# A macaron encoder layer on one core: the moved sums and split remainders of both FFNs, and half of three quarters of a modulation product

## The chip, the cores and the metric

The kernel runs on one core of a Trainium2 chip. The metric is the device time of one execution in microseconds (us); lower is better. Five engines work side by side, each through its own list of instructions in order: PE (TensorE, matrix products), DVE (VectorE), ACT (ScalarE), POOL (GpSimd) and SP (SyncE, which issues most transfers). An engine that waits for something holds up all that stands behind in its own list.

## The reference

One encoder layer over 1024 tokens of width 1024, all in float32:

```python
c_act = silu(c)
mod = c_act @ w_ada + b_ada                 # nine vectors of 1024: shift, scale, gate for three blocks
h = modulate(rms_norm(x, g_ffn1), sh_f1, sc_f1)
x = x + 0.5 * gt_f1 * swiglu(h, w1_gu, w1_down)     # FFN 1, width 2816
h = modulate(rms_norm(x, g_mix), sh_m, sc_m)
...                                          # two attentions with 8 heads each
x = x + gt_m * (o @ w_out)
h = modulate(rms_norm(x, g_ffn2), sh_f2, sc_f2)
x = x + 0.5 * gt_f2 * swiglu(h, w2_gu, w2_down)     # FFN 2
return rms_norm(x, g_final)
```

where `swiglu(h) = (silu(a) * b) @ w_down` with `a, b` the halves of `h @ w_gu`.

## The kernel before

**Precision.** A float32 product is made of three faster ones: each operand is split in a high part (ACT casts it, `Stream.split` L105 or `split_b` L461) and the remainder (a subtraction, L106 or L462), and PE multiplies high by high, high by low and low by high (L485 to L487 in the gate and up products, L741 to L743 in the down products). So every 128x512 block that PE uses first passes ACT once and DVE or POOL once.

**FFN.** The gate and up products run unit by unit (22 units of 128 columns, `GateUp`), each as a two by two block product with seven block products in place of eight. On the weight side that takes the sums S1 to S4 (`unit_specs`, L426; S1 and S3 on POOL, S2 and S4 on DVE), on the side of the activations the sums T1 to T4 (`build`, L468, L470, L473, L476; the first of each part, L468 and L473, on POOL) and remainders (L462; those of B22 and T4 on POOL). For the down product, the gated results of a pair of units are written to DRAM blocks `g_d` by `g_out`, among them three or four sums on POOL (L521); the ones named A... are stored through SP and the ones named S... through POOL's own transfer queue (L517). Of the 22 units, 8 are early: two of their products (A11 with B11, A12 with B21, 24 matrix instructions a unit) are made ahead, while the activations are still being built (`early`, `early2`, `early_rest`); the other five follow in `run`.

**Order of the work.** `Stream` holds a list of weight loads with the steps on them (sums and splits); `pump(n)` takes the next n steps, with 9 split pairs and 2 raw buffers of 1 MB at a time. `Background` steps generators. The order in which the source issues work is not the order on the engines: a scheduler places each instruction in its engine's list.

**First modulation.** Before FFN 1 can start, its shift and scale are needed: `w_ada01` comes in four quarters q of 2 MB, in two loads each (`raw01`, four buffers). `use01` (L795) multiplies each of eight slices with its value of `cact` and adds it into `acc01[q]` on DVE; `prepare1` (L922) then sums over the partitions with four matrix products against a column of ones into `modp`, from which DVE makes `modB` and `modA` (L926, L927), ACT modulates (L911) and splits, and PE can go on with that quarter. `acc_new` (L894, L895) clears the next accumulator on POOL, once PE has read the buffer's last content, and fetches a row of biases through ACT's queue.

**From gate and up to down.** When `run` ends, the buffers of `gu_pools` are given up and the down product's tiles take their place: the gate row (L397) and x (L990 in FFN 1, L1610 in FFN 2) can be loaded only when the last stores from the old buffers are through. The down product's first operand, A12, is read back from `g_d` in three chunks (L95, `raw<-g_A`), through the same SP list.

Of the kernel before, what the change touches and what calls it, by code (L numbers as in the profile page):

```python
# [19 lines left out]
ALU = mybir.AluOpType  # L20
# [4 lines left out]
P = 128  # L25
D = 1024
S = 1024
KT = D // P
# [155 lines left out]
def encoder_layer(ctx: ExitStack, tc: tile.TileContext, a: dict, out: bass.AP):  # L184
    nc = tc.nc
# [10 lines left out]
    st = Stream(nc, rawp, ring)  # L196
# [42 lines left out]
    ones = const.tile([P, P], F32, name="ones")  # L239
# [5 lines left out]
    cact = const.tile([P, KT], F32, name="cact")  # L245
# [170 lines left out]
    def unit_specs(i, u, early):  # L416

        src = a[f"w{i}_gu"][u // 2, u % 2]
        A = [slice(j * 512, (j + 1) * 512) for j in range(4)]
        tmps = {}  # L420

        def comb(nm, eng, x, y, op):
            def f(raw):
                tmps[nm] = sp.tile([P, 512], F32, tag="S", name="S")
                get = lambda v: tmps[v] if isinstance(v, str) else raw[:, A[v]]
                eng.tensor_tensor(tmps[nm], get(x), get(y), op=op)  # L426
            return f

        def blk(nm, v):
            if isinstance(v, str):  # L430
                return ((i, u, nm), None, lambda raw: tmps[v])
            return ((i, u, nm), A[v], None)

        direct = not early
        steps = [comb("S1", nc.gpsimd, 2, 3, ALU.add), comb("S3", nc.gpsimd, 0, 2, ALU.subtract)]
        if direct:
            steps.append(blk("A11", 0))
        steps += [comb("S2", nc.vector, "S1", 0, ALU.subtract), blk("S2", "S2"), blk("S1", "S1"), blk("S3", "S3")]
        if direct:
            steps.append(blk("A12", 1))  # L440
        steps += [comb("S4", nc.vector, 1, "S2", ALU.subtract), blk("S4", "S4"), blk("A22", 3)]
        return [(src, steps)]
# [3 lines left out]
    class GateUp:  # L446
# [17 lines left out]
        def build(self, hf, kk, part):  # L464

            b11, b21, b12, b22 = hf[0][:, kk, :], hf[0][:, kk + 4, :], hf[1][:, kk, :], hf[1][:, kk + 4, :]
            if part == 0:
                nc.gpsimd.tensor_tensor(b11, b12, b11, op=ALU.subtract)  # L468
                self.split_b("T1", kk, b11, nc.vector)
                nc.vector.tensor_tensor(b11, b22, b11, op=ALU.subtract)  # L470
                self.split_b("T2", kk, b11, nc.vector)
            else:
                nc.gpsimd.tensor_tensor(b12, b22, b12, op=ALU.subtract)  # L473
                self.split_b("T3", kk, b12, nc.vector)
                self.split_b("B22", kk, b22, nc.gpsimd)
                nc.vector.tensor_tensor(b21, b21, b11, op=ALU.subtract)  # L476
                self.split_b("T4", kk, b21, nc.gpsimd)

        def prod(self, p, u, wn, bn, kks, start, stop):
            wh, wl = st.get((self.i, u, wn))  # L480
# [31 lines left out]
        def g_out(self, fp, nm):  # L512

            g = self.g

            def put(nm):
                (nc.sync if nm[0] == "A" else nc.gpsimd).dma_start(g_d[nm][:, fp, :], g[nm])  # L517

            def comb(nm, x, y, op, into=None):
                g[nm] = gtp["g"]() if into is None else g[into]  # L520
                nc.gpsimd.tensor_tensor(g[nm], g[x], g[y], op=op)  # L521
                put(nm)

            if nm != "A21":
                put(nm)
            if nm == "A11":
                comb("S3", "A11", "A21", ALU.subtract)
            if nm == "A22":
                comb("S1", "A21", "A22", ALU.add, "A21")
                comb("S2", "S1", "A11", ALU.subtract, "A11")  # L530
                comb("S4", "A12", "S2", ALU.subtract, "A12")
# [18 lines left out]
        def early_rest(self, builds):  # L550

            K4 = (0, 1, 2, 3)
            for u0 in range(NQ0, NE, 4):
                us = range(u0, u0 + 4)
                for u in us:
                    self.bank[u] = ps1()
                    self.prod(self.bank[u], u, "A11", "B11", K4, True, True)
                    self.store_p1(u)
                    next(builds, None)
                    st.pump(2)  # L560
                    bg.step()
                for u in us:
                    self.prod(self.bank[u], u, "A12", "B21", K4, False, True)
                    self.early_out(u)
                    next(builds, None)
                    st.pump(2)
                    bg.step()
            for _ in builds:
                pass
# [219 lines left out]

    acc01 = {}  # L790

    def use01(q, kt):
        def use(raw):
            ac = acc01[q]
            nc.vector.scalar_tensor_tensor(out=ac, in0=raw[:, kt % 4 * 512:(kt % 4 + 1) * 512], scalar=cact[:, kt:kt + 1],  # L795
                                           in1=ac, op0=ALU.mult, op1=ALU.add)
        return use
# [63 lines left out]
    x = [xs.tile([P, D], F32, name=f"x{t}") for t in range(NT)]  # L861
# [37 lines left out]
    modp = p1p.tile([P, 512], F32, tag="ps1", name="modp")  # L899
# [14 lines left out]
    def prepare1(q):  # L914
        if q == 1:
            for t in range(4, 8):
                bg.spawn(start_gen(t))
                bg.step()
        st.upto(ends01[q] + (1 if q < 2 else 0))
        p = modp[:, 4 * q:4 * q + 4]  # L920
        for m in range(4):
            nc.tensor.matmul(p[:, m:m + 1], acc01[q][:, m * P:(m + 1) * P], ones[:, 0:1], start=True, stop=True)  # L922
        if q < 2:
            acc_new(q + 2)
        ks = slice(2 * q, 2 * q + 2)
        nc.vector.tensor_copy(modB[0][:, ks], p[:, 0:2])  # L926
        nc.vector.scalar_tensor_tensor(out=modA[0][:, ks], in0=p[:, 2:4], scalar=1.0,  # L927
                                       in1=cols[:, C_GF1 + 2 * q:C_GF1 + 2 * q + 2], op0=ALU.add, op1=ALU.mult)
        for k in (2 * q, 2 * q + 1):
            modulate(0, k)  # L930
            ffn.split_b("B11" if k < 4 else "B21", k % 4, hf[0][:, k, :], nc.vector)
        if q == 3:
            bg.finish()
            ss_.close()
            R2.append(rs.enter_context(tc.tile_pool(name="R2", bufs=1, side="right")))
            ffn.alloc(R2[0], T_NAMES)
            st.hold, st.hold_step = hold_u0 + 1, hold_u0


            def builds():  # L940
                for part in range(2):
                    for kk in range(4):
                        if part == 0:
                            modulate(1, kk)
                            modulate(1, kk + 4)
                        ffn.build(hf, kk, part)
                        yield

            return builds()
# [33 lines left out]
    x = [dp.tile([P, D], F32, name=f"x{t}") for t in range(NT)]  # L983
# [45 lines left out]
    for t in range(NT):  # L1029
        bg.finish(norms[t])  # L1030
        p = in_proj(t, "b", 256)
# [391 lines left out]
    for s in range(NQ + LAG + 3):  # L1423
        if s < NQ:
            i, t = divmod(s, NT)
            p = scores(i, t)
# [304 lines left out]
```

## Time and profile before

| | |
|---|---|
| median of 3 runs | 2048.51 us (2046.16 to 2048.94) |
| profiled execution, its own time | 2049.28 us |
| its span | 2047.5 us |
| mean granted clock of TensorE | 0.988 of full speed |
| PE busy | 1971.7 us (96%) |
| DVE busy | 1540.1 us (75%) |
| ACT busy | 973.4 us (48%) |
| POOL busy | 483.7 us (24%) |

The shares are averages over stages of different kinds: FFN 1 until about 700 us, the projections and attentions until about 1380, FFN 2 to the end. What a change is worth in one of them is read from that stage: where PE has no gap, work on another engine is hidden, and where PE waits, the last wait counts. [...]

### The profile page before, as it was taken

The numbers are of one execution on the slowest core, as the hardware profiler recorded it, in microseconds if no ns is written. First come the engines' busy times: TensorE is split into PE (matmuls) and PEld (weight loads), VectorE is DVE, ScalarE is ACT, GpSimd is POOL, SyncE is SP. The second block draws the span as 40 slices with busy tenths as digits, with TensorE's granted clock in tenths as the row PEclk, the third lists the DMA queues.
The fourth block names the chain that finished last, engine by engine and source line by source line (L and its number), as shares of the span: only waits on it lengthen the run. The fifth ranks groups of instructions, "written<-read, shape, count | busy, mean of one in ns | idle before, by whom it ended". The sixth has DMA issues, their size and how long they took to land. (4 is left out here: it accounts for less than half of the span.)

```text
span 2047.5 us, 28023 instructions
## 1 busy us (share of the span) xinstructions
PE 1971.7 (96%) x10301; PEld 1678.1 (82%) x10301; DVE 1540.1 (75%) x2381; ACT 973.4 (48%) x1865; POOL 483.7 (24%) x428
## 2 busy tenths in 40 slices
PE   6889999999999999999999999998999999999998
PEld 5678888887788888798989998996788888877886
DVE  7898689886697776788888778667776555547976
ACT  6522322322344653677787777467323333324444
POOL 1544344433000032212200000005343332320011
PEclk9999999999999999999999999998999999999999
DMA  8275366565832334523253330433442332358223
GB/s 344 88 246 186 106 202 216 197 223 187 334 116 93 147 123 143 156 63 118 89 165 83 83 75 30 164 127 126 165 163 100 113 118 83 113 207 322 98 93 118
DMA packets 90550, 303.30 MB, mean 148 GB/s; under 512 B 9848, under 2 KB 22427, under 8 KB 76588
## 3 DMA queue, kind: packets, MB, share of 16 engines
q1 hardware_dynamic: 81018, 274.21, 39.8%
q0 software_dynamic: 7040, 23.07, 2.9%
q10 hardware_dynamic: 2354, 4.22, 0.5%
q8 instruction: 81, 1.33, 0.3%
q14 instruction: 57, 0.47, 0.1%
HBM read 220.98 MB, written 80.49 MB: 147 GB/s over the span
## 5 line engine op out<-in xcount | busy, mean ns | idle before, releaser
L105 ACT CAST uh<-raw 128x512 fp32r<-128x512 f32 (+1 forms) x343 | 210.4, 622 | 228.8 <-PE ps L486 148.1
L106 DVE TENSOR_TENSOR ul<-raw,uh 128x512 fp32r<-128x512 f32 (+1 forms) x343 | 250.3, 735 | 41.1 <-ACT uh L105 40.7
L105 ACT CAST uh<-S 128x512 fp32r<-128x512 f32 x198 | 121.6, 621 | 302.3 <-PE ps L486 234.7
L741 PE MATMUL ps<-uh 128*128 128x512 f32 x616 | 240.8, 393 | 7.3 <-ACT uh L105 7.3
L742 PE MATMUL ps<-ul,uh 128*128 128x512 f32 x616 | 241.5, 392 | 1.7 <-DVE ul L106 1.7
L743 PE MATMUL ps<-uh,ul 128*128 128x512 f32 x616 | 240.9, 391 | 0.0
L1428 DVE TENSOR_REDUCE nm<-ps 128x1 f32<-128x1024 f32 x128 | 155.7, 1216 | 70.6 <-PE ps L223 40.9
L106 DVE TENSOR_TENSOR ul<-S,uh 128x512 fp32r<-128x512 f32 x198 | 168.8, 858 | 41.8 <-ACT uh L105 41.6
L521 POOL TENSOR_TENSOR g<-g 128x512 f32<-128x512 f32 x88 | 135.1, 1535 | 244.3 <-DVE g L508 243.3
L1446 ACT CAST ph<-ps 128x512 fp32r<-128x512 f32 x256 | 138.0, 590 | 79.6 <-PE ps L1445 79.4
L426 POOL TENSOR_TENSOR S<-raw 128x512 f32<-128x512 f32 x88 | 123.4, 1414 | 200.3 <-DMA raw<-in_w_gu_dram 122.5
L1456 DVE TENSOR_TENSOR pl<-ps,ph 128x512 fp32r<-128x512 f32 x256 | 163.9, 683 | 0.0
L1451 ACT ACTIVATE pe<-ps,nm 128x1024 f32<-128x1024 f32 x128 | 143.6, 1122 | 17.2 <-DVE nm L1428 17.1
L741 PEld LDWEIGHTS ps<-uh 128*128 128x128 f32 x616 | 116.1, 189 | 33.2 <-ACT uh L105 9.0
L742 PEld LDWEIGHTS ps<-ul,uh 128*128 128x128 f32 x616 | 116.4, 189 | 27.7 <-DVE ul L106 3.8
L743 PEld LDWEIGHTS ps<-uh,ul 128*128 128x128 f32 x616 | 116.3, 189 | 24.2
L1445 PE MATMUL ps<-ident,pe 128*128 128x128 f32 x1024 | 134.9, 273 | 0.8 <-DVE pl L1456 0.4
L1445 PEld LDWEIGHTS ps<-ident,pe 128*128 128x128 f32 x1024 | 119.7, 141 | 19.0 <-DVE pl L1456 0.6
L105 ACT CAST uh<-hT 128x512 fp32r<-128x512 f32 x96 | 59.7, 622 | 150.4 <-PE ps L742 113.5
L1394 PE MATMUL po<-ph,V 128*128 128x256 f32 x512 | 129.7, 291 | 0.0
L1395 PE MATMUL po<-pl,V 128*128 128x256 f32 x512 | 125.9, 283 | 0.0
L233 POOL TENSOR_TENSOR r<-v,neghalf 128x1 f32<-128x1 f32 x32 | 26.0, 813 | 363.8 <-DVE v L229 363.8
(280 smaller groups left out, 5178.0 us busy)
## 6 DMA issues: line engine op xcount, KB each, us to landing
raw<-in_w_gu_dram SPq DMA_DIRECT2D x52, 1024.0 KB
ada<-in_w_ada_dram SPq DMA_DIRECT2D x56, 512.0 KB
g_S<-g POOLq DMA_DIRECT2D x88, 256.0 KB, 2.6
g_A<-g SPq DMA_DIRECT2D x66, 256.0 KB
hT<-in_w_down_dram SPq DMA_DIRECT2D x16, 1024.0 KB
raw<-g_S SPq DMA_DIRECT2D x16, 1024.0 KB
raw<-g_A SPq DMA_DIRECT2D x12, 1024.0 KB
x<-in_x_dram SPq DMA_DIRECT2D x16, 512.0 KB
```

The costliest lines, as they stand in the source:

```text
L105: nc.scalar.copy(hi[:, 0:n], ap)
L106: nc.vector.tensor_tensor(lo[:, 0:n], ap, f32(hi[:, 0:n]), op=ALU.subtract)
L521: nc.gpsimd.tensor_tensor(g[nm], g[x], g[y], op=op)
L741: nc.tensor.matmul(p, gh[:, tsl], wh, start=start, stop=False, skip_group_check=True)
L742: nc.tensor.matmul(p, gh[:, tsl], wl, start=False, stop=False, skip_group_check=True)
L743: nc.tensor.matmul(p, gl[:, tsl], wh, start=False, stop=stop, skip_group_check=True)
L1394: nc.tensor.matmul(po[:, 0:256], V, gr.ph[:, k, :], start=(k == 0), stop=False)
L1428: nc.vector.tensor_reduce(nm, p, axis=AX.X, op=ALU.max, negate=True)
L1445: nc.tensor.transpose(out=pt[:, k, :], in_=pe[:, (4 * n + k) * P:(4 * n + k + 1) * P], identity=ident)
L1446: nc.scalar.copy(gr.ph[:, 4 * n:4 * n + 4, es], pt)
L1451: nc.scalar.activation(pe, p, AF.Exp, bias=nm, accum_out=ls[:, s % 2:s % 2 + 1])
L1456: nc.vector.tensor_tensor(gr.pl[:, nsl, es], pts[n], f32(gr.ph[:, nsl, es]), op=ALU.subtract)
```

## The change

1. The sums S1 and S3 (L426), the sums of `g_out` (L521), the first sums of `build` (L468, L473) and the remainders of B22 and T4 (L462) move from POOL to DVE. POOL keeps clearing tiles, the powers of `inv_rms`, its stores and what it does in the attentions.
2. In `early_rest`, the step on the weights (`st.pump(2)`) comes ahead of the step on the activations (`next(builds, None)`).
3. Of quarters 1 to 3 of the first modulation, DVE adds up the first four slices only. For the last four a new function `mod_matmuls` multiplies the raw block by four columns of `cact` on PE (16 products of 128x128 by one column), with the four products against ones in between. The buffers `raw01` are given back by PE there, not by DVE.

```diff
-        steps = [comb("S1", nc.gpsimd, 2, 3, ALU.add), comb("S3", nc.gpsimd, 0, 2, ALU.subtract)]
+        steps = [comb("S1", nc.vector, 2, 3, ALU.add), comb("S3", nc.vector, 0, 2, ALU.subtract)]
...
             if part == 0:
-                nc.gpsimd.tensor_tensor(b11, b12, b11, op=ALU.subtract)
+                nc.vector.tensor_tensor(b11, b12, b11, op=ALU.subtract)
...
             else:
-                nc.gpsimd.tensor_tensor(b12, b22, b12, op=ALU.subtract)
+                nc.vector.tensor_tensor(b12, b22, b12, op=ALU.subtract)
                 self.split_b("T3", kk, b12, nc.vector)
-                self.split_b("B22", kk, b22, nc.gpsimd)
+                self.split_b("B22", kk, b22, nc.vector)
                 nc.vector.tensor_tensor(b21, b21, b11, op=ALU.subtract)
-                self.split_b("T4", kk, b21, nc.gpsimd)
+                self.split_b("T4", kk, b21, nc.vector)
...
                 g[nm] = gtp["g"]() if into is None else g[into]
-                nc.gpsimd.tensor_tensor(g[nm], g[x], g[y], op=op)
+                nc.vector.tensor_tensor(g[nm], g[x], g[y], op=op)
...
                     self.store_p1(u)
+                    st.pump(2)
                     next(builds, None)
-                    st.pump(2)
...
                     self.early_out(u)
+                    st.pump(2)
                     next(builds, None)
-                    st.pump(2)
...
+    def mod_matmuls(q, raw=None):
+
+        for m in range(4):
+            ms = slice(m * P, (m + 1) * P)
+            o = modp[:, 4 * q + m:4 * q + m + 1]
+            if raw is not None:
+                for j in range(4):
+                    nc.tensor.matmul(o, raw[:, j * 512:(j + 1) * 512][:, ms], cact[:, 4 + j:5 + j], start=j == 0, stop=False)
+            nc.tensor.matmul(o, acc01[q][:, ms], ones[:, 0:1], start=raw is None, stop=True)
+
     def use01(q, kt):
         def use(raw):
+            if q and kt >= 4:
+                if kt == KT - 1:
+                    mod_matmuls(q, raw)
+                return
...
-        for m in range(4):
-            nc.tensor.matmul(p[:, m:m + 1], acc01[q][:, m * P:(m + 1) * P], ones[:, 0:1], start=True, stop=True)
+        if q == 0:
+            mod_matmuls(0)
```

The scheduler places other instructions anew as well. Three places show it. First, PE's list behind the first twelve products of FFN 1 (`ps_268` is the second unit's bank, `modp` the modulation's, `ps_345` takes transposed x). Before:

```order
L487 MATMUL ps_268<-B11h_128,ul 128x512
L922 MATMUL modp<-ones,acc 128x1 x4
L882 MATMUL ps_345<-ident,xn 128x128 x4
L485 MATMUL ps_269<-B11h_128,uh 128x512
```

With the change:

```order
L487 MATMUL ps_268<-B11h_128,ul 128x512
L799 MATMUL modp<-cact,raw_177 128x1 x4
L800 MATMUL modp<-ones,acc 128x1
L799 MATMUL modp<-cact,raw_177 128x1 x4
L800 MATMUL modp<-ones,acc 128x1
L799 MATMUL modp<-cact,raw_177 128x1 x4
L800 MATMUL modp<-ones,acc 128x1
L799 MATMUL modp<-cact,raw_177 128x1 x4
L800 MATMUL modp<-ones,acc 128x1
L896 MATMUL ps_345<-ident,xn 128x128 x4
```

Twenty products stand where four stood. They stand again in front of the quarters 2 and 3; in quarter 2 the last six products of the unit before and four groups of transposes moved behind them.

Second, DVE's list while FFN 2's activations are built (T1l to T4l and B22l are remainders, `hT` the sums, `eg` an early unit's result, which frees a bank for PE). Before, between the second and the third `eg`:

```order
L508 TENSOR_TENSOR eg<-ps_14637,es 128x512
L462 TENSOR_TENSOR T2l_14598<-hT,T2h_14597 128x512
L106 TENSOR_TENSOR ul<-raw,uh 128x512
L462 TENSOR_TENSOR T3l_14600<-hT,T3h_14599 128x512
L462 TENSOR_TENSOR T3l_14602<-hT,T3h_14601 128x512
L476 TENSOR_TENSOR hT<-hT 128x512 x2
L426 TENSOR_TENSOR S<-S,raw 128x512
L426 TENSOR_TENSOR S<-raw,S 128x512
L462 TENSOR_TENSOR T3l_14602<-hT,T3h_14601 128x512
L106 TENSOR_TENSOR ul<-S,uh 128x512 x4
L106 TENSOR_TENSOR ul<-raw,uh 128x512
```

With the change, the end of that stretch:

```order
L462 TENSOR_TENSOR T3l_14638<-hT,T3h_14637 128x512
L462 TENSOR_TENSOR B22l_14626<-hT,B22h_14625 128x512
L462 TENSOR_TENSOR T4l_14642<-hT,T4h_14641 128x512
L476 TENSOR_TENSOR hT<-hT 128x512
L426 TENSOR_TENSOR S<-raw 128x512 x2
L462 TENSOR_TENSOR T4l_14642<-hT,T4h_14641 128x512
L426 TENSOR_TENSOR S<-S,raw 128x512
L508 TENSOR_TENSOR eg<-ps_14827,es 128x512
L426 TENSOR_TENSOR S<-raw,S 128x512
L106 TENSOR_TENSOR ul<-S,uh 128x512 x4
L106 TENSOR_TENSOR ul<-raw,uh 128x512
```

The remainders and sums from POOL stand between the others, and the third `eg` now stands ahead of the five splits that it stood behind.

Third, SP's list where FFN 2 goes from the gate and up products to the down product (`g_A_93` is A12, `g_A_92` A11). Before:

```order
L86 DMA hT<-in_w_down_dram 128x2048
L397 DMA gate<-gd 128x1024
L1610 DMA z_17968<-xd_91 128x1024
L1610 DMA z_17969<-xd_91 128x1024
L1610 DMA z_17970<-xd_91 128x1024
L1610 DMA z_17971<-xd_91 128x1024
L95 DMA raw<-g_A_93 128x1536
L95 DMA raw<-g_A_92 128x2048
```

With the change:

```order
L86 DMA hT<-in_w_down_dram 128x2048
L95 DMA raw<-g_A_93 128x1536
L397 DMA gate<-gd 128x1024
L1624 DMA z_18004<-xd_91 128x1024
L1624 DMA z_18005<-xd_91 128x1024
L1624 DMA z_18006<-xd_91 128x1024
L1624 DMA z_18007<-xd_91 128x1024
L95 DMA raw<-g_A_92 128x2048 x2
```

The third chunk of A12 moved from behind the gate row and four rows of x to ahead of them; in FFN 1 it moved in the same way.

## Rows read from the trace of the kernel before

**Rows 1.** Windows: us, then each engine's busy time (instructions), PEclk, DMA share, GB/s.

```profile
50.00:100.00 50.00, 40.20 (x155) 30.00 (x156) 44.69 (x47) 31.55 (x56) 27.48 (x18) 0.90 0.21 75
100.00:150.00 50.00, 43.60 (x184) 35.10 (x184) 45.30 (x54) 12.38 (x22) 20.71 (x18) 0.96 0.71 243
150.00:480.00 330.00, 330.00 (x1471) 271.57 (x1470) 270.74 (x328) 101.08 (x171) 137.65 (x112) 1.00 0.57 190
...
496.00:530.00 34.00, 29.69 (x121) 22.94 (x120) 19.96 (x28) 14.04 (x26) 7.83 (x8) 0.95 0.84 316
...
1396.00:1450.00 54.00, 43.66 (x169) 34.30 (x168) 48.48 (x47) 27.62 (x52) 33.82 (x22) 0.87 0.34 118
...
1450.00:1820.00 370.00, 370.00 (x1634) 306.35 (x1634) 223.25 (x316) 111.58 (x183) 127.82 (x119) 1.00 0.35 121
...
1820.00:1852.00 32.00, 27.32 (x110) 21.15 (x109) 18.60 (x26) 13.00 (x24) 7.51 (x8) 0.95 0.82 312
```

**Rows 2.** Shorter windows in the first modulation and FFN 2's building stage, same columns.

```profile
51.00:57.00 6.00, 5.12 (x11) 3.23 (x12) 5.89 (x7) 3.94 (x7) 3.76 (x3) 0.51 0.11 44
...
1423.00:1428.00 5.00, 5.00 (x12) 3.94 (x13) 5.00 (x4) 1.45 (x3) 4.06 (x3) 0.50 0.77 254
1431.00:1436.00 5.00, 5.00 (x22) 4.17 (x23) 5.00 (x5) 3.60 (x7) 4.37 (x3) 1.00 0.33 99
1442.00:1446.40 4.40, 4.40 (x12) 3.46 (x13) 1.30 (x3) 0.03 (x1) 1.88 (x2) 0.61 0.65 251
```

**Rows 3.** Timeline, PE: start, duration, instruction, in brackets idle time before.

```profile
51.84 1.65 PE L485 MATMUL ps<-B21h,uh 128*128 128x512 f32 x3 [2.82 <-ACT B21h L461]
...
84.58 0.79 PE L487 MATMUL ps<-B21h,ul 128*128 128x512 f32 x1 [3.91 <-DVE ul L106]
...
1422.98 0.79 PE L485 MATMUL ps<-B21h,uh 128*128 128x512 f32 x1 [6.21 <-ACT c L493]
...
1847.62 0.50 PE L741 MATMUL ps<-uh 128*128 128x512 f32 x1 [3.32 <-ACT uh L105]
```

**Rows 4.** Timeline, DVE in FFN 2's building stage.

```profile
1398.25 2.65 DVE L106 TENSOR_TENSOR ul<-raw,uh 128x512 fp32r<-128x512 f32 x2 [9.02 <-ACT uh L105]
...
1408.23 0.68 DVE L462 TENSOR_TENSOR T1l<-hT,T1h 128x512 fp32r<-128x512 f32 x1
...
1413.19 1.78 DVE L462 TENSOR_TENSOR T1l<-hT,T1h 128x512 fp32r<-128x512 f32 x1
...
1432.74 5.78 DVE L106 TENSOR_TENSOR ul<-S,uh 128x512 fp32r<-128x512 f32 x4
...
1439.64 0.68 DVE L508 TENSOR_TENSOR eg<-ps,es 128x512 f32<-128x512 f32 x1
```

**Rows 5.** Costliest groups: line, instruction, count | busy us, mean ns | idle before.

```profile
L106 DVE TENSOR_TENSOR ul<-S,uh 128x512 fp32r<-128x512 f32 x198 | 168.8, 858 | 41.8 <-ACT uh L105 41.6
L521 POOL TENSOR_TENSOR g<-g 128x512 f32<-128x512 f32 x88 | 135.1, 1535 | 244.3 <-DVE g L508 243.3
...
L426 POOL TENSOR_TENSOR S<-raw 128x512 f32<-128x512 f32 x88 | 123.4, 1414 | 200.3 <-DMA raw<-in_w_gu_dram 122.5
```

**Rows 6.** Timelines of DVE, PE and POOL in the first modulation.

```profile
18.77 2.49 DVE L106 TENSOR_TENSOR ul<-raw,uh 128x512 fp32r<-128x512 f32 x4
...
29.39 1.03 PE L922 MATMUL modp<-ones,acc 128*128 128x1 f32 x8
...
30.48 0.52 POOL L894 MEMSET acc<- 128x512 f32 x1 [9.12 <-PE modp L922]
```

**Rows 7.** Timeline, SP (issue times), and the transfers of 1826 to 1850.

```profile
1835.84 1.11 SPq L95 DMA_DIRECT2D raw<-g_A  x2
...
DMA packets 1612, 7.46 MB, mean 311 GB/s; under 512 B 208, under 2 KB 208, under 8 KB 1232
```

**Rows 8.** Waits of POOL and DVE: us in total, times, longest.

```profile
POOL S L426 <- DMA raw<-in_w_gu_dram: 122.5, 18, 11.7
...
DVE acc L313 <- DMA ada<-in_w_ada_dram: 11.1, 6, 4.3
```

## Prediction

> **What bounds the kernel now.** I read the windows first, because a share over the whole execution mixes stages. In the steady part of both FFNs PE works without a gap: 330.00 of 330 us from 150 to 480 and 370.00 of 370 us from 1450 to 1820, at clock 1.00, while DVE and POOL both have idle time [rows 1]. Whatever another engine does there is hidden. PE loses time only at the edges of these runs. From 50 to 150 it is idle 9.80 + 6.40 = 16.20 us, from 1396 to 1450 it is idle 10.34 us, and at the two passages from gate and up to down (496 to 530, 1820 to 1852) 4.31 and 4.68 us. In these windows DVE is busy for 44.69 of 50, 45.30 of 50 and 48.48 of 54 us [rows 1], so there it is nearly a bound itself.
>
> A gap costs more than its length. [...] I count the missing clock of a window as lost time too: 5.00 x 0.50 = 2.5 us there, 4.40 x 0.39 = 1.7 us from 1442, 6.00 x 0.49 = 2.9 us from 51 to 57 [rows 2].
>
> Next, why DVE is slow there. The timeline shows the same remainder (T1l) with 0.68 us at 1408.23 and 1.78 us at 1413.19, and four splits of S in 5.78 us at 1432.74 [rows 4], where four splits early in the program take 2.49 us [rows 6], 0.62 each. POOL's sums take 1414 and 1535 ns each over the whole execution, and the splits of S 858 ns on average [rows 5]. So both engines read as slower while both work. One sum moved to DVE takes some 1.4 us from POOL, adds 0.62 us to DVE, and takes away a neighbour that makes DVE's own work nearly three times as long.
>
> **The change part by part.** The sum is made against the profiled execution's 2049.28 us, which is 0.77 above the median.
>
> *Steady runs: 0.* With everything on DVE, 328 + 112 instructions x 0.62 = 273 of 330 us and 316 + 119 x 0.62 = 270 of 370 us [rows 1, 6] (an upper estimate, as some of POOL's instructions stay). DVE stays under 85%, and what hides its work is PE's full list. If DVE were held up there by over 15% of the stage, PE would run dry; that is rival D.
>
> *FFN 2's building stage (1396 to 1450): -12.* PE can gain 10.34 us of idle time and 2.5 + 1.7 of clock, 14.5 in all. DVE's list up to the third `eg` has 40 instructions in the new order; at 0.62 that is 24.8 us, so it ends near 1425 when it begins at 1400, where it stood at 1439.64 [rows 4]. The second edit helps here too: splits of weights stand ahead of the activations' steps. PE's 96 products of the four units before need 5.00 / 22 = 0.227 us each [rows 2], 21.8 us, so from 1407 PE is busy until 1429 and finds that bank free. I keep 2.5 us as lost: DVE begins the stage late (its first splits wait 9.02 us for ACT's cast [rows 4]). Bounds: the gap at 1422.98 waits for ACT, not DVE; if it stays with its clock, 14.5 - 6.2 - 2.5 = 5.8 are left, so -6; at the other end -14.5.
>
> *FFN 1's building stage (50 to 150): -11.* Idle time without the part before 51.84 (which belongs to the next term) is 16.20 - 1.84 = 14.4 us; missing clock is 50 x 0.10 + 50 x 0.04 - 2.9 = 4.1 us [rows 1, 2]; together 18.5. The largest gap, 3.91 us at 84.58, waits for DVE's `ul` [rows 3]. If DVE sets the pace, the gain is its own: it is busy 89.99 us, and 47 + 54 of its instructions and all 36 of POOL's at 0.62 are 85 [rows 1, 6], so -5; if PE does, -18.5. DVE is neither full nor idle here, so I take -11, near the middle.
>
> *First modulation: +7.* The change takes 4 additions from DVE in each of three quarters, which only helps DVE and is in the term above. It adds 3 x 16 products to PE. Four products stand as eight records in the timeline and take 1.03 us [rows 6], 0.129 each, so 96 records are 12.4 us. In quarter 1 they stand where PE waits 2.82 us for `B21h` before 51.84 [rows 3] and then runs 51 to 57 at clock 0.51 [rows 2]. I count the wait as filled and the clock as kept for all but half a microsecond: 12.4 - 2.8 - 2.4 = +7. At one end nothing is filled, because the quarter's raw block lands late and the products come after the wait: +12.4. At the other, quarters 2 and 3 also fill half of the 14.4 us of waits in FFN 1's stage: about 0. Here a wait moves: the raw buffers are now given back by PE, and the next load of quarter 3 stands behind that in SP's list. From 50 to 100 the DMA share is 0.21 [rows 1], so a megabyte finds room, and I cost it at nothing; without that room, 1 MB at the 311 GB/s of rows 7 is 3.4 us. Clearing `acc` on POOL waits 9.12 us for `modp` already [rows 6], and ACT's bias row and DVE's `modB` stand behind; a quarter whose PE products take 5 us in place of 1 delays both by 4 us, and that is inside the +12.4.
>
> *The two passages to down: -9.5.* Each loses its idle time and 5% of clock: 4.31 + 1.7 and 4.68 + 1.6, 12.3 in all [rows 1]. The gap of 3.32 us at 1847.62 [rows 3] waits for the cast of the third chunk of A12, issued at 1835.84 [rows 7], after a gate row and four rows of x. These rows are 128x1024 in float32, 2.6 MB; at 311 GB/s [rows 7] they take 8.4 us of transfer that now comes after the chunk. That is over twice the gap, so the gap goes; small waits of 0.3 to 0.6 us remain, about 1.4 us a passage. The gate row and x are late next, but the down product needs them only at its end. Also, the last sums of `g_out` leave POOL, where one takes 1.5 us. Bounds: only half of the wait goes, -5, or everything, -12.3.
>
> Sum: 0 - 12 - 11 + 7 - 9.5 = -25.5, so 2049.28 - 25.5 = **2023.8 us**. All ends at their worst give -6 - 5 + 12.4 - 5 = -3.6 (2045.7), all at their best -14.5 - 18.5 + 0 - 12.3 = -45.3 (2004.0).
>
> [...]
>
> **The rivals.**
> - *B: the modulation eats half.* PE waits in FFN 1's stage because DVE is the pace, and the new products come on top of it: +12.4 and only -5 there, the rest as forecast: -12 - 5 + 12.4 - 9.5 = -14.1, 2035. For it: DVE is busy for 90% of both windows [rows 1]. Against it: its 101 instructions there are 63 us at 0.62; the other 27 of its 90 us come from the work beside POOL.
> - *C: the building stages are bound by ACT.* The largest gap names a cast of ACT [rows 3], and ACT runs in order too. Then both stages keep their waits, and only the passages gain: -9.5 + 7 = -2.5, 2046.8. Against it: ACT is busy for 27.62 of 54 us [rows 1], so it waits for others, and what it waits for is DVE.
> - *D: slower, through waits for raw weights at the head of DVE's list.* POOL's sums S1 and S3 wait 122.5 us for `in_w_gu`, 18 times, up to 11.7 us [rows 8]. On POOL that hurt few. On DVE the splits, the gated results and the bank releases stand behind such a wait. It decides once a load lands more than some 4.3 us after DVE has come to its sum; that is the longest wait for a load that DVE already has, in the steady part, where PE stays full [rows 8]. Price: 122.5 - 18 x 4.3 = 45 us; 2023.8 + 45 = 2069. Against it: POOL waits long because it is ahead of PE, with little to do, and DVE comes later to the same sum. A load rate of 190 and 121 GB/s in the steady windows [rows 1] leaves room.
> - *E: the change does less than it says*, since the scheduler places everything anew, and the new lists give up elsewhere what they gain here. The new order has no such piece in the steady runs; I add its chance to C's.
>
> **How the numbers follow.** About 0.2%, 4.1 us, is what a measurement of this kernel can tell from no change. The forecast (2008 to 2033, by its bounds, taken as not all at one end) gets 0.64, B 0.22, C with E 0.07, D 0.07. The range takes in the forecast and B: **2008 to 2040**, which leaves C, D and the far ends out. Chances: faster 0.64 + 0.22 = 0.86 and 0.01 of C, 0.87; the same 0.06; slower 0.07.
>
> **What would show it right or wrong.** No sums of L426 and L521 are left on POOL; the splits of S have a mean near 0.65 us, not 0.858. From 1396 to 1450 PE's idle time falls from 10.34 to under 4 us, and the third `eg` comes some 25 us after the first splits. From 50 to 150 idle time falls by 8 or more, and each of three quarters shows some 5 us of `modp`. The third chunk of A12 is issued ahead of the gate row and the gap before the first down product is under 1 us. PE stays full in the long windows. The forecast is wrong if DVE waits for `in_w_gu` behind which PE stands idle in the steady runs (D), if PE's gap at the third `eg` stays and still names ACT (C), or if `modp` itself waits for the raw block and PE with it (B).

## The result, and the profile after

| | before | with the change |
|---|---|---|
| median | 2048.73 us (2046.16 to 2049.21, 4 runs) | 2016.30 us (2014.03 to 2019.09, 4 runs) |
| ratio | | 0.9845, 95% interval 0.9828 to 0.9862 |
| profiled execution, its span | 2049.28, 2047.5 us | 2014.90, 2013.1 us |

The change makes the kernel 1.55% faster, some 32 us; the forecast was 25.5 us (2023.8) with a range of 2008 to 2040. To see where the time went I cut both executions at the same places in PE's work: the first starts of the products of L485, L741 and L221, which the views of these lines give. A column is the time from one such place to the next.

| span in us | start to FFN 1's first down product | to the first product of the projections (L221) | to FFN 2's first product (L485) | FFN 2, gate and up | to the end | sum |
|---|---|---|---|---|---|---|
| before | 498.0 | 221.4 | 662.6 | 439.3 | 226.2 | 2047.5 |
| with the change | 491.2 | 215.3 | 663.0 | 423.2 | 220.4 | 2013.1 |
| difference | -6.8 | -6.1 | +0.4 | -16.1 | -5.8 | -34.4 |

Half of the gain lies in FFN 2's gate and up, a third in the two passages to down, and a fifth ahead of FFN 1's first down product. The windows of the changed kernel (columns as in rows 1: PE, PEld, DVE, ACT, POOL busy, granted clock, DMA share, GB/s) answer to [rows 1]; the stretches 1383:1437, 489:523 and 1790:1822 are those of 1396:1450, 496:530 and 1820:1852, moved by what was gained ahead of them:

```profile
50.00:100.00 50.00, 49.11 (x225) 40.57 (x226) 33.72 (x58) 31.73 (x56) 0.00 (x0) 0.86 0.24 85
100.00:150.00 50.00, 48.21 (x214) 39.59 (x213) 49.40 (x79) 19.46 (x34) 3.33 (x5) 1.00 0.65 217
150.00:480.00 330.00, 330.00 (x1477) 272.07 (x1476) 272.56 (x394) 99.70 (x167) 25.20 (x42) 1.00 0.57 194
1383.00:1437.00 54.00, 54.00 (x240) 44.69 (x239) 51.41 (x85) 33.38 (x62) 0.00 (x0) 1.00 0.44 152
1437.00:1780.00 343.00, 343.00 (x1515) 284.12 (x1514) 237.88 (x371) 105.79 (x174) 21.72 (x40) 1.00 0.34 121
489.00:523.00 34.00, 33.78 (x148) 27.39 (x147) 22.61 (x37) 16.54 (x30) 2.17 (x4) 1.00 0.93 356
1790.00:1822.00 32.00, 31.65 (x139) 25.45 (x138) 20.51 (x34) 14.89 (x28) 2.17 (x4) 1.00 0.91 355
```

FFN 2's building stage, idle for 10.34 us before, has no gap at all: 54.00 of 54 at clock 1.00. DVE starts 85 instructions there in 51.41 us, where it took 48.48 us for 47. From 150 to 480 it starts 394 instead of 328 in nearly the same busy time (272.56 against 270.74), because each is shorter. PE's idle time from 50 to 150 fell as well, from 16.20 to 0.89 + 1.79 = 2.68 us, and yet the stretch to FFN 1's first down product became only 6.8 us shorter: the new products fill part of that time, and from 50 to 100 the clock is 0.86. In the costliest groups (answering to [rows 5]):

```profile
L106 DVE TENSOR_TENSOR ul<-S,uh 128x512 fp32r<-128x512 f32 x198 | 134.5, 685 | 34.6 <-ACT uh L105 34.4
...
L521 DVE TENSOR_TENSOR g<-g 128x512 f32<-128x512 f32 x88 | 60.4, 686 | 1.0 <-DMA g_A<-g 0.3
...
L426 DVE TENSOR_TENSOR S<-raw 128x512 f32<-128x512 f32 x88 | 59.5, 688 | 15.7 <-DMA raw<-in_w_gu_dram 14.4
```

The splits of S have a mean of 685 ns, not 858. The two groups of sums, 258.5 us on POOL before, take 119.9 us on DVE. DVE's timeline in FFN 2's building stage answers to [rows 4]:

```profile
1385.93 0.68 DVE L106 TENSOR_TENSOR ul<-raw,uh 128x512 fp32r<-128x512 f32 x1
...
1387.13 0.68 DVE L106 TENSOR_TENSOR ul<-raw,uh 128x512 fp32r<-128x512 f32 x1
...
1400.98 0.68 DVE L508 TENSOR_TENSOR eg<-ps,es 128x512 f32<-128x512 f32 x1
...
1411.63 0.68 DVE L508 TENSOR_TENSOR eg<-ps,es 128x512 f32<-128x512 f32 x1
```

From 1387.13 to 1400.98 lie 23 starts, 0.602 us apart: a duration of 0.68 overlaps the next start. The third `eg` comes at 1411.63, 25.7 us after the first of these splits (25 were forecast). SP's list at the second passage (issue times) has the chunk first, as the order said, and answers to [rows 7]. PE's wait for that chunk, 3.32 us before, is gone; the longest waits that are left in the two passages are 0.22 and 0.35 us. The list:

```profile
1799.50 0.33 SPq L95 DMA_DIRECT2D raw<-g_A  x1
1806.58 0.33 SPq L397 DMA_DIRECT2D gate<-gd  x1
1806.96 1.95 SPq L1624 DMA_DIRECT2D z<-xd  x4
```

DVE's own wait for raw weights answers to [rows 8], where POOL waited 122.5 us in 18 waits of up to 11.7:

```profile
DVE S L426 <- DMA raw<-in_w_gu_dram: 14.4, 13, 4.1
```

What went the other way is the first modulation. Windows of the changed kernel over the products of quarter 1, then of quarter 2 and of quarter 3, these two with the stretch behind them:

```profile
28.60:34.80 6.20, 6.19 (x41) 6.09 (x39) 0.00 (x0) 0.00 (x0) 0.00 (x0) 0.71 1.02 423
...
47.70:52.40 4.70, 4.70 (x42) 4.70 (x41) 0.75 (x1) 0.82 (x2) 0.00 (x0) 0.92 0.30 113
52.40:57.50 5.10, 4.23 (x14) 3.12 (x14) 2.39 (x5) 2.54 (x5) 0.00 (x0) 0.50 0.00 0
...
64.20:68.60 4.40, 4.40 (x41) 4.37 (x40) 0.66 (x1) 1.29 (x2) 0.00 (x0) 1.00 0.15 60
68.60:73.00 4.40, 4.40 (x14) 3.49 (x14) 2.72 (x7) 3.95 (x7) 0.00 (x0) 0.61 0.00 0
```

PE is never idle while it makes the one-column products (twenty products, forty records a quarter), and yet the granted clock is 0.71 over those of quarter 1 and 0.50 and 0.61 behind those of quarters 2 and 3. DVE, ACT and POOL stand nearly still while these products run.

### The profile page after: what moved, and what is told of

Its sections match the earlier page's. It is cut to its first block, busy times and chain, and to the rows that moved or that the text cites. A ratio compares the mean times of both kernels' runs of the same rounds, so it can differ in the third digit from the quotient of the medians.

```text
span 2013.1 us, 28104 instructions
## 1 busy us (share of the span) xinstructions
PE 1969.9 (98%) x10397; PEld 1686.4 (84%) x10397; DVE 1546.2 (77%) x2577; ACT 974.9 (48%) x1865; POOL 171.3 (9%) x220
## 4 chain that ended last, share of the span: by engine, by line
PE 92%; ACT 3%; DVE 2%; DMA 1%; issue 1%; POOL 0%; SPq 0%; POOLq 0%; ACTq 0%; DVEq 0%
PE ps L485 14%; PE ps L486 14%; PE ps L487 14%; PE ps L742 7%; PE ps L741 7%; PE ps L743 7%; PE ps L1459 5%; PE ps L221 5%; PE ps L223 5%; PE ps L222 5%; PE po L1408 3%; PE po L1409 3%; PE ps L1392 1%; PE ps L1393 1%; ACT h L374 1%
## 5 line engine op out<-in xcount | busy, mean ns | idle before, releaser
L106 DVE TENSOR_TENSOR ul<-raw,uh 128x512 fp32r<-128x512 f32 (+1 forms) x343 | 235.0, 691 | 34.5 <-ACT uh L105 34.2
L741 PE MATMUL ps<-uh 128*128 128x512 f32 x616 | 238.3, 390 | 0.6 <-ACT uh L105 0.6
L106 DVE TENSOR_TENSOR ul<-S,uh 128x512 fp32r<-128x512 f32 x198 | 134.5, 685 | 34.6 <-ACT uh L105 34.4
L741 PEld LDWEIGHTS ps<-uh 128*128 128x128 f32 x616 | 115.5, 188 | 25.3 <-ACT uh L105 1.4
L517 POOL DMA_DIRECT2D g_S<-g x88 | 47.9, 544 | 667.5 <-DVE g L521 596.6
L1408 PEld LDWEIGHTS po<-ph,V 128*128 128x128 f32 x512 | 97.4, 190 | 2.1
L1409 PEld LDWEIGHTS po<-pl,V 128*128 128x128 f32 x512 | 97.8, 191 | 0.2
```

Of the source, the lines that this page charges most:

```text
L106: nc.vector.tensor_tensor(lo[:, 0:n], ap, f32(hi[:, 0:n]), op=ALU.subtract)
L741: nc.tensor.matmul(p, gh[:, tsl], wh, start=start, stop=False, skip_group_check=True)
L1408: nc.tensor.matmul(po[:, 0:256], V, gr.ph[:, k, :], start=(k == 0), stop=False)
L1409: nc.tensor.matmul(po[:, 0:256], V, gr.pl[:, k, :], start=False, stop=(k == NT - 1))
```

## The experiments

Each was timed beside the kernel before on the same chip (medians of that kernel from 2047.06 to 2048.37 us); compare kernels that ran on different chips by their ratios. The stages, cut as above:

| kernel | median, ratio (95% interval) | start to down 1 | to L221 | to FFN 2 | gate and up 2 | to the end |
|---|---|---|---|---|---|---|
| with the change | 2016.30, 0.9845 (0.9828 to 0.9862) | 491.2 | 215.3 | 663.0 | 423.2 | 220.4 |
| mod_dve | 2003.50, 0.9783 (0.9768 to 0.9797) | 480.7 | 215.3 | 662.6 | 423.2 | 220.2 |
| only_mod | 2058.58, 1.0054 (1.0037 to 1.0071) | 509.7 | 222.5 | 663.7 | 439.1 | 224.1 |
| mod_q3 | 2007.74, 0.9800 (0.9786 to 0.9815) | 484.0 | 215.3 | 663.0 | 423.2 | 220.2 |
| ghost | 2031.54, 0.9920 (0.9905 to 0.9935) | 490.2 | 215.3 | 663.5 | 438.5 | 220.5 |
| ghost_copy | 2022.07, 0.9868 (0.9850 to 0.9886) | 491.2 | 215.2 | 663.4 | 429.7 | 220.3 |
| b_pool | 2033.75, 0.9936 (0.9921 to 0.9951) | 497.1 | 215.4 | 663.5 | 435.0 | 219.9 |
| s_pool | 2022.87, 0.9879 (0.9865 to 0.9894) | 498.8 | 215.2 | 663.6 | 424.4 | 219.7 |
| g_pool | 2025.15, 0.9890 (0.9874 to 0.9907) | 490.9 | 219.9 | 663.2 | 423.2 | 222.7 |
| g_late | 2018.80, 0.9856 (0.9840 to 0.9873) | 495.5 | 216.1 | 663.6 | 423.4 | 220.3 |
| no_swap | 2016.65, 0.9851 (0.9836 to 0.9866) | 490.8 | 215.3 | 663.0 | 424.5 | 219.8 |
| mod_dve_noswap | 2001.76, 0.9769 (0.9752 to 0.9787) | 478.3 | 215.0 | 662.8 | 422.9 | 220.1 |

### Work on POOL that nobody needs

```diff
+                if ghost and nm in ("S1", "S3"):
+                    nc.gpsimd.tensor_tensor(ghost[0], raw[:, A[x]], raw[:, A[y]], op=op)
...
+                if ghost:
+                    for _ in range(3):
+                        nc.gpsimd.tensor_tensor(ghost[0], b22, b22, op=ALU.subtract)
```

> The changed kernel, and while FFN 2's activations are built POOL does work again that nobody needs: it repeats S1 and S3 into a scratch tile, and four subtractions of two 128x512 operands for each of the four blocks. DVE still makes everything that is used, and waits for none of it. My theory (what the move takes away is the slowing of DVE beside POOL): DVE's 128x512 subtractions in that stage read 1.2 to 1.8 us again where POOL works, PE gets idle time of 5 to 12 us back in that stage, and the time is 2022 to 2032. Rival (what counted was waiting for POOL's own slow results): DVE's subtractions stay at 0.6 to 0.7 us, PE has no gap there, and the time is 2014 to 2018.

The trace has no repeated S1 or S3: the scratch tile is written by four and twelve subtractions, all from 1383.28 to 1407.35, and by nothing else. The kernel took 15.2 us more than the changed kernel, and 15.3 of its profile's lie in FFN 2's gate and up. Its timelines of POOL, DVE and PE in that stage:

```profile
1383.28 6.71 POOL L476 TENSOR_TENSOR ghost<-hT 128x512 f32<-128x512 f32 x4 [7.81 <-ACT hT L374]
1390.07 17.28 POOL L485 TENSOR_TENSOR ghost<-hT 128x512 f32<-128x512 f32 x12
...
1393.36 1.53 DVE L465 TENSOR_TENSOR T1l<-hT,T1h 128x512 fp32r<-128x512 f32 x1
...
1404.93 0.68 DVE L516 TENSOR_TENSOR eg<-ps,es 128x512 f32<-128x512 f32 x1
...
1407.83 0.68 DVE L465 TENSOR_TENSOR T1l<-hT,T1h 128x512 fp32r<-128x512 f32 x1
...
1400.39 0.79 PE L493 MATMUL ps<-B11h,uh 128*128 128x512 f32 x1 [5.64 <-ACT es L510]
```

While POOL runs (until 1407.35), T1l takes 1.53 us; just behind its end, 0.68. DVE uses none of POOL's results, and the trace has no wait of DVE for POOL in this stage. PE gets a gap of 5.64 us that, once more, names ACT. So the slowing of DVE beside POOL is the cause, and sixteen subtractions that nobody needs give back nearly all of FFN 2's 16.1 us. Two details: POOL's twelve take 17.28 / 12 = 1.44 us each, and DVE's instructions beside them start 1.45 us apart (1393.36 to 1394.81), one for one; and `eg`, which has one operand in PSUM, keeps its 0.68 at 1404.93 in the middle of this.

The same with copies of one operand, at all three places:

```diff
-                        nc.gpsimd.tensor_tensor(ghost[0], b22, b22, op=ALU.subtract)
+                        nc.gpsimd.tensor_copy(ghost[0], b22)
```

> As the run with useless work on POOL, but with copies of one 128x512 operand in place of sums of two. My theory (POOL slows DVE by reading and writing the same memory, whatever the operation): DVE's subtractions read over 1 us beside them, PE gets gaps of 3 to 12 us in FFN 2's building stage, 2020 to 2032. Rival (only two operands on both sides collide): DVE's subtractions stay at 0.6 to 0.7 us, 2014 to 2019.

```profile
1388.02 12.31 POOL L485 COPY ghost<-hT 128x512 f32<-128x512 f32 x12
```

```profile
1391.47 1.09 DVE L478 TENSOR_TENSOR hT<-hT 128x512 f32<-128x512 f32 x1
...
1398.58 0.68 DVE L516 TENSOR_TENSOR eg<-ps,es 128x512 f32<-128x512 f32 x1
```

DVE reads 1.09 us, with starts 1.02 apart, and POOL's copies take about as long (12.31 / 12 = 1.03). The stage is 6.5 us longer, and PE's longest gap in it is 2.98 us, just under the 3 that I had expected. So the copies with one operand slowed DVE too, and by less than the sums: 1.02 us from start to start, where it was 1.45.

Side by side, the readings are 1.45 us from start to start beside POOL's sums, 1.02 beside its copies, and a duration of 0.68 for the instruction with an operand in PSUM in both runs. What the operand in PSUM changes, and which of the two engines holds up the other, they don't tell.

### Which of the moves carries the gain

> Only the first sums of build (L468, L473) and the remainders of B22 and T4 go back to POOL, 16 instructions in each FFN's building stage. My theory (they slow DVE beside them where DVE is nearly the bound): DVE's subtractions read 1.2 to 1.8 us beside them, gaps come back in FFN 2's building stage and in FFN 1's, and the time is 2024 to 2040. Rival (POOL as a helper takes work from DVE and costs nothing): 2012 to 2018.

```diff
-                nc.vector.tensor_tensor(b11, b12, b11, op=ALU.subtract)
+                nc.gpsimd.tensor_tensor(b11, b12, b11, op=ALU.subtract)
...
-                self.split_b("T4", kk, b21, nc.vector)
+                self.split_b("T4", kk, b21, nc.gpsimd)
```

(and L473 and B22 in the same way.) The kernel is 17.5 us slower than the changed one: 11.8 in FFN 2's gate and up and 5.9 up to FFN 1's down product. In its window and DVE's timeline the old picture is back (two instructions in 3.47 us, PE idle for 8.58 of 55):

```profile
1385.00:1440.00 55.00, 46.42 (x194) 36.54 (x193) 46.60 (x54) 32.48 (x65) 27.66 (x16) 0.97 0.37 128
```

```profile
1414.29 3.47 DVE L462 TENSOR_TENSOR T3l<-hT,T3h 128x512 fp32r<-128x512 f32 x2
```

> Only S1 and S3 (88 sums) go back to POOL. My theory: nearly all of them lie in the steady runs, where PE is full, and only the few in the building stages count: 2015 to 2023, the long windows full. Rival D of the prediction (their waits for raw weights hold up DVE's list): it would get faster, 2005 to 2013. Another rival (DVE is slowed in the steady runs until PE runs dry): over 2026.

```diff
-        steps = [comb("S1", nc.vector, 2, 3, ALU.add), comb("S3", nc.vector, 0, 2, ALU.subtract)]
+        steps = [comb("S1", nc.gpsimd, 2, 3, ALU.add), comb("S3", nc.gpsimd, 0, 2, ALU.subtract)]
```

The kernel is 6.6 us slower than the changed one, with 7.6 of its profile's up to FFN 1's down product and 1.2 in FFN 2's gate and up. In FFN 2's steady run the rest of the 88 sums costs nothing on either engine (PE is busy for 340.00 of 340 us from 1450 to 1790); in FFN 1's PE is idle for 1.89 us of 330 from 150 to 480, so that long window isn't quite full, though I had expected it to be. Rival D would have made this kernel faster; it fell.

> The second part of the change is undone: the step on the activations comes ahead of the step on the weights again; all else is as in the changed kernel. My theory (the gain is DVE freed of POOL as a neighbour, the order is worth little): 2013 to 2020, no gap over 1 us in FFN 2's building stage. Rival (the weights' splits have to come first, or PE waits for them): a gap of 3 us or more there, and 2021 to 2030.

```diff
-                    st.pump(2)
                     next(builds, None)
+                    st.pump(2)
```

(at both places.) 2016.65 against 2016.30: the second part of the change does nothing that can be measured here, though the order of steps was given part of the first term.

### The passages

> Of the change, only the sums of g_out (L521) go back to POOL. With this alone the scheduler puts the third chunk of A12 behind the gate row and four rows of x again, as before the change. My theory (the passages are lost to that order): a gap of about 3 us comes back before the first down products, some 5 to 6 us for each passage, and the time is 2024 to 2029, while the long windows stay full and the building stages stay as they are. Rival 1 (these sums don't matter, because PE is the bound everywhere): 2014 to 2019. Rival 2 (DVE is slowed beside POOL until PE runs dry in the steady runs): over 2032, with gaps there.

```diff
-                nc.vector.tensor_tensor(g[nm], g[x], g[y], op=op)
+                nc.gpsimd.tensor_tensor(g[nm], g[x], g[y], op=op)
```

> As the run before it, with L521 on POOL, but the gate row and the first four rows of x are issued after the fourth step of the down product, so that the third chunk of A12 stands ahead of them in SP's list. My theory (the order in SP's list makes the passage's gap): the gaps before the first down products are under 1 us and the time is 2014 to 2019. Rival (the gap comes from POOL's late sums and stores, not from the order): gaps of 2 to 3 us stay and the time is 2022 to 2029.

```diff
-    gate = bcast_row(dp, gd[0], "gate")
+    gate = dp.tile([P, gd[0].shape[0]], F32, name="gate", bufs=1)
...
-    x_load(range(4, 8))
...
+        if j == -1:
+            nc.sync.dma_start(gate, gd[0].partition_broadcast(P))
+            x_load(range(4, 8))
...
+                if j == 0 and k == 4:
+                    before(-1)
```

(and the same in FFN 2.) With L521 on POOL the passages are 4.6 and 2.3 us longer (the columns "to L221" and "to the end"), less than the 5 to 6 that I had expected, and the steady runs are unchanged. PE waits again in both, though for 1.27 and 1.30 us and not 3; in FFN 1's passage, with the chunk (the first of the two `raw<-g_A`) behind the gate row and x in SP's list, these are the wait, PE's window around it, and the list:

```profile
515.33 0.49 PE L741 MATMUL ps<-uh 128*128 128x512 f32 x1 [1.27 <-ACT uh L105]
```

```profile
516.00:521.00 5.00, 4.87 (x14) 3.89 (x15) 4.34 (x9) 3.62 (x8) 0.00 (x0) 0.66 0.77 275
```

```profile
502.64 0.33 SPq L397 DMA_DIRECT2D gate<-gd  x1
503.02 2.02 SPq L1004 DMA_DIRECT2D x<-in_x_dram  x4
505.14 1.06 SPq L95 DMA_DIRECT2D raw<-g_A  x2
```

The wait is not all of the 4.6 us: PE is idle for 2.18 us from 490.9 to 521, where the changed kernel's PE has no gap from 491.2 on, and behind the wait the clock is 0.66 over 5 us, another 1.7. With the chunk ahead and the sums still on POOL the passages are back at 216.1 and 220.3 us, 6.2 less in all, no wait of PE at their beginning is over 0.60 us, and the median fell by 6.35. So it is SP's order that makes the passage, not POOL's late sums. The profiles as a whole differ by only 1.0 us, because g_late's lost 4.6 us up to FFN 1's first down product against g_pool's. The rows give part of it as clock (0.87 and 0.97 from 50 to 100 and from 100 to 150, against 0.93 and 1.00); why stays open.

### The modulation

> The third part of the change is undone: all eight slices of each quarter are added up on DVE again; the moves from POOL to DVE and the new order stay. My theory (the products on PE lie on the path at the start and cost about 6 us there): the first B21 product starts near 52 instead of 57.5 us, PE's idle time from 50 to 150 stays under 6 us, and the time is about 2010 (2007 to 2014). Rival (the relief of DVE is what lets FFN 1's building stage go through): B21 waits for DVE, PE's idle time from 50 to 150 rises above 8 us, and the time is 2019 to 2026.

```diff
-            if q and kt >= 4:
+            if q in MODQ and kt >= 4:
...
-        if q == 0:
-            mod_matmuls(0)
+        if q not in MODQ:
+            mod_matmuls(q)
```

with `MODQ = ()`. The kernel is 12.8 us faster than the changed one, more than I had expected (2007 to 2014); PE's idle time from 50 to 150 is 2.50 us, under the 6 that I had expected. PE's first transposes behind quarter 1 and its first B21 product, in the changed kernel and then in this one:

```profile
36.83 1.09 PE L896 MATMUL ps<-ident,xn 128*128 128x128 f32 x4 [2.03 <-DVE xn L889]
...
57.52 1.22 PE L485 MATMUL ps<-B21h,uh 128*128 128x512 f32 x2 [0.89 <-ACT B21h L461]
```

```profile
32.84 1.08 PE L897 MATMUL ps<-ident,xn 128*128 128x128 f32 x4 [2.93 <-DVE v L229]
...
51.35 1.61 PE L485 MATMUL ps<-B21h,uh 128*128 128x512 f32 x3 [2.38 <-ACT B21h L461]
```

Quarter 1's products cost 4.0 us, those of quarter 2 bring it to 6.2, as expected, and a further 4.3 us come until FFN 1's first down product (10.5 in all). Windows of this kernel where the changed one had clock 0.84 and 0.73:

```profile
60.00:66.00 6.00, 6.00 (x28) 4.96 (x27) 6.00 (x11) 5.91 (x11) 0.00 (x0) 1.00 0.00 0
66.00:72.00 6.00, 6.00 (x27) 4.82 (x27) 5.71 (x10) 5.37 (x11) 0.00 (x0) 1.00 0.35 134
```

DVE is full or nearly so here, PE has no gap, and the clock stays at 1.00: the additions fit on DVE.

> The kernel before with the third part of the change alone. My theory, after the run without it (the products stand on the path whole and the clock falls behind them): 2055 to 2062 against the kernel before's 2047 to 2049, first B21 product some 6 us later than 51.8. Rival (they fall into waits that are there anyway, and DVE gets the relief it needs in FFN 1's building stage): 2040 to 2050.

(The kernel before with `mod_matmuls` and the new `use01`.) It is 10.2 us slower than the kernel before; 11.7 of its profile's lie ahead of FFN 1's down product. Its first B21 product starts at 58.95 us instead of 51.84, 7.1 later where I had expected some 6. PE's idle time from 50 to 150 fell from 16.20 to 8.38 us, but its clock there fell from 0.93 to 0.86. So on a kernel where PE has 14 us of waits in that stage the products do fill some of them, and the stage is 11.7 us longer all the same.

> The products of the modulation on PE for the last quarter only; quarters 1 and 2 are added up on DVE. My theory (each quarter's sixteen products lie on the path and lower the clock behind them, about 4 us a quarter): 2006 to 2010, between 2003.5 without any and 2016.3 with three. Rival (only quarters 1 and 2 cost, because the start waits for them, and the last one is hidden): 2001 to 2004.

(`MODQ = (3,)`.) It takes 4.2 us more than mod_dve, about a third of what three quarters cost. The products stand in another place than in the changed kernel, at 49.00 us, right behind quarter 2's four. These are the windows of the products and of the stretch behind them:

```profile
48.80:56.20 7.40, 6.33 (x41) 6.25 (x42) 2.07 (x5) 2.55 (x4) 0.00 (x0) 0.77 0.09 35
56.20:60.60 4.40, 4.40 (x13) 3.40 (x14) 3.48 (x8) 4.11 (x7) 0.00 (x0) 0.60 0.00 0
```

### The first part of the change alone

> The first part of the change alone: the work moved from POOL to DVE, the order in the building stages and the modulation as before the change. My theory (this part is the whole gain): 2001 to 2007, about 43 us under the kernel before, PE without a gap over 1 us in FFN 2's building stage. Rival (without the products on PE, DVE has so much to do that the order decides): gaps of 2 us or more behind late splits of weights, 2009 to 2018.

This is mod_dve and no_swap together, and the lowest median of all: 2001.76 us, 0.9769 of the kernel before (0.9752 to 0.9787), 14.5 us under the change as it was made. The interval overlaps that of mod_dve, so the two can't be told apart. Its windows of the building stages:

```profile
50.00:100.00 50.00, 47.18 (x199) 37.14 (x200) 46.51 (x78) 33.59 (x60) 0.95 (x1) 0.97 0.43 151
100.00:150.00 50.00, 50.00 (x223) 41.41 (x222) 48.01 (x75) 16.95 (x29) 2.91 (x5) 1.00 0.61 209
1365.00:1450.00 85.00, 85.00 (x378) 70.45 (x377) 73.40 (x120) 45.68 (x88) 2.24 (x4) 1.00 0.46 159
```

## Why the prediction was right, and where it was off

The direction and the main mechanism (DVE freed of POOL beside it) held, and the time lies in the range; the gain was 34.4 us in the profiles against a sum of 25.5. In part that is luck: three gains were forecast too small, and a price that was forecast too small as well took some of that back. By its terms:

- **Steady runs, 0.** Held: 330.00 of 330 and 343.00 of 343. DVE's busy time was forecast as at most 273 of 330 and is 272.56; that it comes so near is chance, as DVE makes 394 instructions there and not 440, at 0.69 us and not 0.62.
- **FFN 2's building stage, -12.** Measured -16.1, over the end of -14.5. The mechanism is shown (ghost). Of the 4.1 us that the forecast missed, 2.5 are the loss kept for DVE's late start, which did not come. The clock was a little small, too: I had added up two windows in [rows 2], 1423 to 1428 at 0.50 and 1442 to 1446.4 at 0.61, 2.5 + 1.7 us, where the mean clock of 0.87 over 54 us in [rows 1] gives 7.0 us. Of these, 2.1 lie in PE's longest gap (6.30 x 0.34, first row below) and are counted as idle time already. So 10.34 + 4.9 = 15.2 us were there to gain; where the last 0.9 came from, the rows don't show. The second part of the change, which this term counted as a help, gave nothing that can be measured (no_swap).
- **FFN 1's building stage, -11, and first modulation, +7.** Together -4 was forecast and -6.8 measured, but both were too small. Without the products on PE the stretch gains 17.3 us (498.0 to 480.7), near the end of -18.5: it was PE's lost time that came back, not only DVE's own. The products cost 10.5 us on top of that, and 11.7 on the kernel before, near the end of +12.4. Their own time was forecast well: 6.2, 4.9 and 4.5 us less three times the 1.03 of the old four products is 12.5. The step that failed is "I count the wait as filled and the clock as kept". The wait of 2.82 us before the first B21 product, which the prediction put in quarter 1, lies behind the products of quarter 2, and there it did shrink, to 0.89. But quarter 1's products lie ahead of it, from 28.62 to 34.79 us, and there a wait of 2.03 us stays behind them where it was 2.51; DVE makes `modB` only after all of a quarter's products, and waited 3.92 us for them in quarters 2 and 3; and the clock fell (to 0.50 and 0.61 behind quarters 2 and 3) although PE was never idle while it made them.
- **The passages, -9.5.** Measured -6.1 and -5.8, -11.9, near the end of -12.3. The order in SP's list is shown to be the lever (g_pool against g_late).
- **Rivals.** B: its price for the products came near (10.5 of 12.4), but not its pace: of PE's two waits from 50 to 150, 0.89 and 1.79 us, none is for DVE. C: the gap named ACT before, and names it again in the ghost run, where only DVE was slowed; ACT was waiting itself, in the kernel before from 1396 to 1450 most of all for DVE's sums (second row below). D: DVE waits 14.4 us for raw weights, at most 4.1 at once, just under the 4.3 from which I let it decide, with PE full; so POOL's 122.5 us for the same sums were mostly the waits of an engine that came to them early. E: outside the stages of the change the new lists gave up at most 0.4 us (663.0 against 662.6).
- **The price of one instruction on DVE, 0.62.** The splits of S have a mean duration of 685 ns where I had expected near 650; the starts lie 0.602 us apart, and the third `eg` came 25.7 us after the first split, where 40 instructions at 0.62 make 24.8. The price was near, though the row was not quite rightly read: four in 2.49 us are three starts of 0.60 and one duration of 0.68, so the price is 0.60 and not 0.62, and DVE makes 42 instructions in that stretch, not 40.

The two rows of the kernel before: the window of PE's longest gap in FFN 2's building stage (columns as in rows 1), and ACT's longest wait from 1396 to 1450 (us in total, times, longest).

```profile
1416.70:1423.00 6.30, 0.09 (x2) 0.02 (x1) 6.30 (x9) 4.39 (x9) 2.68 (x2) 0.66 0.03 11
```

```profile
ACT T2h L461 <- DVE hT L470: 10.6, 4, 4.1
```

## What to carry to other kernels

Before you give a helper engine part of an elementwise load, look at the same instruction of the main engine with and without it beside: here one sum on POOL cost DVE 1.45 - 0.60 = 0.85 us, more than the 0.60 of doing that sum itself. Where an engine is full only at the edges of a long run, read idle time and missing clock of just these windows; take the missing clock of all the time in which the engine works, not only of the windows in which you noticed it, and not of its idle time, which is counted already. Don't count small products that relieve another engine as free on the bounding one, even in a stage with gaps (here they cost 10.5 us, and 11.7 on the kernel before): ask what waits for their result, and read the clock behind them.

## What was not expected of the hardware

The granted clock fell behind stretches in which PE was busy throughout with one-column products: the mean is 0.50 from 52.40 to 57.50 behind 4.70 of 4.70 us busy at 0.92, and 0.61 from 68.60 to 73.00 behind 4.40 of 4.40 us busy at 1.00. It is 0.60 behind the same products in the run with one quarter, where PE had been idle for 1.07 of 7.40 us as well. In this case a list of such products left the clock as PE's gap of 6.21 us did in the kernel before (0.50 from 1423 to 1428). Beside POOL, DVE's subtractions with two operands in SBUF started in step with POOL's instructions (1.45 us beside sums, 1.02 beside copies, 0.602 alone), while one with an operand in PSUM kept its 0.68.
